# Half of the inner index of two column groups of each output projection by seven half products

## The chip, the cores and the metric

The kernel runs on one core of one Trainium2 chip. The metric is the time of one execution on the device in microseconds (us); the time before is the median of three runs. Profiled executions are taken separately; the trace of one of them gives every time below that isn't called a median.

## What is computed

The reference is a decoder trunk of two layers on 256 tokens of width 2048 in float32. Layer 0 mixes the tokens by gated linear attention, layer 1 by attention over a sliding window; each also attends to 256 memory tokens, and each has an MLP of width 8192:

```python
for i in range(DEPTH):
    h = rmsnorm(x, attn_norm_g[i])
...
    x = x + jnp.concatenate([o_mix, o_mem], axis=-1) @ w_out[i]
    x = x + squared_relu_mlp(rmsnorm(x, mlp_norm_g[i]), w_up[i], w_down[i])
return rmsnorm(x, final_norm_g)
```

Here `o_mix` is 256 x 1536, from the layer's mixer, and `o_mem` 256 x 512, from the memory; `DEPTH` is 2. The change concerns the product with `w_out[i]`: 256 tokens, an inner index of 2048 and 2048 columns.

## The kernel before

All weights pass through a list of *items*, made layer by layer (projections of the mixer, `out_halves`, `mlp_halves`). An item is one 128 x 1024 block of weights in float32 with the matmuls that use it. The main loop walks the list with a lead: at item i, SP issues the load of item i+13 (`load`, into one of eight buffers `wr`), item i+7 may add blocks on DVE (`prep`), and item i+5 is split (`split`, L1141): ACT copies the block in reduced precision to `wh` (L1152), DVE writes the rest to `wl` (L1153). There are six buffers, here called slots, for each of `wh` and `wl`. Then come late tasks (normalisations, adds into `x`) and the item's own matmuls. A matmul product is made of three: high by high, high by low, low by high, each 128x512.

The engines run their own queues in order. The order that stands in each queue is fixed when the program is built, from the order of this code and a scheduler's own model of times; a buffer's next writer waits for its last reader, whichever comes last.

`out_halves` (L805) makes the output projection in four column groups g of 512 columns, each of eight items (parts) of two chunks of the inner index, that is 2 token tiles x 2 chunks x 3 = 12 matmuls. The order is group 0 parts 0 to 5, group 1 parts 0 to 5, the rest of both, then group 2 and group 3. The left operands are `os0` to `os15`, high and low parts of the attention's output. `OUT_ROWS` gives the order of the chunks. When a group has ended, `add_residual` (L772) adds its two accumulators into x (`x02` is token tile 0, group 2) on DVE (L774), and `norm_task` begins the norm that the MLP needs.

The MLP's `down_fast` already uses seven products in place of eight for its down projection: for a 2 x 2 arrangement of blocks (token tiles by inner halves, and inner halves by column groups) it multiplies operands made on DVE by sums of weight blocks, in an order given by `FAST` (L61), and adds the results into x with signs (each entry: left operand, name, accumulator, whether it is that accumulator's first, and the uses):

```python
A21, A11, A22, A12, S3, GG, S2, S4 = range(8)
FAST = [(A11, "B11", 0, True, [(0, 0, 1)]),
        (GG, "T1", 1, True, [(1, 1, -1)]),
        (S2, "T2", 0, False, [(0, 1, -1)]),
        (S4, "B22", 1, False, [(0, 1, -1)]),
        (S3, "T3", 0, False, [(1, 1, -1)]),
        (A12, "B21", 1, True, [(0, 0, 1)]),
        (A22, "T4", 0, False, [(1, 0, 1)])]
```

T1 to T4 are sums of blocks: a room `sum` takes B11, gets B12 added (T1), then B22 (T2) and B21 (T4) by loads that POOL issues and that add in place; a room `b12` takes B12 and gets B22 added for T3. A *half product* is one such product for one half of its inner part (u=0 or 1): two chunks, six matmuls.

The names in the attention's phase: `mk` and `mv` hold the memory's keys and values, `v` the mixer's values in layer 0, `wp` and `wpt` attention weights in layer 1.

Of the kernel before, what the change touches and what calls it, by code (L numbers as in the profile page):

```python
# [10 lines left out]
F32 = mybir.dt.float32  # L11
F32R = mybir.dt.float32r
AF = mybir.ActivationFunctionType
ALU = mybir.AluOpType
# [56 lines left out]
WOVEN_MEM = [3, 3, 2, 2, 2, 1, 0]  # L71

# [17 lines left out]
def trunk_kernel(ctx: ExitStack, tc: tile.TileContext, a, out):  # L90
# [358 lines left out]
    def gla_halves():  # L449
        hs = []  # L450

        def v_done(g):
            def f(accs):
                if g == 0:
                    S["v"] = S["phase"].pool.tile([P, 2, 1536], F32, name="v")
                for t in range(2):
                    w = min(388, 1536 - g * 388)
                    act.activation(S["v"][:, t, g * 388:g * 388 + w], accs[t][:, 0:w], AF.Copy,
                                   scale=S["st"].tok[:, t:t + 1])
                    if w < 388:  # L460
                        act.activation(glr_tok[:, t, 0:16], accs[t][:, w:388], AF.Copy, scale=S["st"].tok[:, t:t + 1])
                if g == 3:
                    tasks.append(gate_task())
            return f
# [81 lines left out]
    def gla_task(h):  # L546
# [57 lines left out]
        for j in range(3):  # L604
            b = bank("aux", f"go{h}{j}")
            col = h * 384 + j * P
            pe.matmul(b[:, 0:T], S["v"][:, 0, col:col + P], at[:, 0:T], start=True, stop=False, skip_group_check=True)
            pe.matmul(b[:, P:T], S["v"][:, 1, col:col + P], at[:, T:T + P], start=False, stop=True,
# [202 lines left out]

    def out_halves(layer):
        hs = []
        for g in range(4):
            def done(accs, g=g):
                add_residual(g, accs)
                tasks.append(norm_task(g, f"mx{layer}", G_MLP + layer))

            hs.append(tm_halves(f"o{layer}{g}", [a["w_out"][layer, g, i] for i in range(8)], 512, lambda: S["os"], done,
                                OUT_ROWS[layer]))  # L820

        return hs[0][0:6] + hs[1][0:6] + hs[0][6:] + hs[1][6:] + hs[2] + hs[3]

    def mlp_halves(layer):
# [5 lines left out]
        def open_phase():  # L830
            S["phase"].close()
            S["phase"] = Phase(f"mlp{layer}")
            S["st"].finish()

        def up(n):
# [3 lines left out]
            def part(i):  # L839
                def mm(wh, wl):  # L840
                    if i == 0:
                        if n == 0:
                            open_phase()
                        st["acc"] = [bank("main" if n < 2 else "aux", f"u{layer}{n}_acc{t}") for t in range(2)]
                    for t in range(2):
                        for k in range(2):
# [4 lines left out]
                            pe.matmul(acc, hi, h, start=2 * i + k == 0, stop=False)  # L851
                            pe.matmul(acc, hi, l, start=False, stop=False)  # L852
                            pe.matmul(acc, lo, h, start=False, stop=2 * i + k == NK - 1)  # L853
                    if i == 7:
# [7 lines left out]
            return [part(i) for i in range(8)]  # L862
# [52 lines left out]
        sums, held = {}, {}  # L915

        def down_fast(e):
# [5 lines left out]
            def item(idx, u, pair):  # L923
                o, name, which, first, uses = FAST[idx]

                def mm(wh, wl):
                    if u == 0 and pair not in sums:
                        sums[pair] = {}
                    if u == 0 and which not in sums[pair]:
                        sums[pair][which] = bank("main", f"d{layer}{e}{pair}{which}")  # L930
                    acc = sums[pair][which]
                    products(acc, 2 * e + u, o, wh, wl, first and u == 0, u == 1)
                    if u == 1:
                        def take():
                            for t, col, sign in uses:
                                dst = x[t][2 * pair + col]
                                if sign > 0:
                                    dve.tensor_tensor(dst, acc, dst, ALU.add)  # L938
                                else:
                                    dve.tensor_tensor(dst, dst, acc, ALU.subtract)  # L940
                                if e == 7 and name in ("T3", "T4"):
                                    tasks.append(norm_end_task(2 * pair + col))
                        later.append([1, take])

                def tile_of(kind):
                    return lambda *_: held[kind, pair, u, e]

                def new(kind):
                    def f():
                        held[kind, pair, u, e] = S["phase"].pool.tile([P, 1024], F32, tag=f"{kind}{pair}{u}",  # L950
                                                                   name=f"{kind}{layer}{e}{pair}{u}")
                        return held[kind, pair, u, e]
                    return f

                def plus(other):
                    return lambda raw: pool_e.dma_start(held["sum", pair, u, e], block(pair, u, other), accum_op=ALU.add)  # L956

                def first_sum():
                    dve.tensor_tensor(held["sum", pair, u, e], held["sum", pair, u, e], held["b12", pair, u, e], ALU.add)

                def third_sum(raw):
                    dve.tensor_tensor(held["b12", pair, u, e], held["b12", pair, u, e], raw, ALU.add)

                if name == "B11":
                    return Item(block(pair, u, "B11"), 1024, mm=mm, into=new("sum"), tile=tile_of("sum"))
                if name == "T1":
                    return Item(block(pair, u, "B12"), 1024, mm=mm, into=new("b12"), tile=tile_of("sum"),
                                prep=first_sum, then=plus("B22"))
                if name == "T2":
                    return Item(None, 1024, mm=mm, tile=tile_of("sum"), then=plus("B21"))  # L970
                if name == "T4":
                    return Item(None, 1024, mm=mm, tile=tile_of("sum"))
                if name == "T3":
                    return Item(None, 1024, mm=mm, tile=tile_of("b12"))
                if name == "B22":
                    return Item(block(pair, u, "B22"), 1024, mm=mm, then=third_sum)
                return Item(block(pair, u, name), 1024, mm=mm)

            return [item(idx, u, pair) for idx in range(7) for u in range(2) for pair in range(2)]


# [107 lines left out]
        def woven(us, ds, counts):  # L1089

            hs = []
            for i, d in enumerate(ds):
                w, j = counts[i // 4], i % 4
                for _ in range((w * (j + 1) + 3) // 4 - (w * j + 3) // 4):
                    hs += us.pop(0)
                hs.append(d)
            return hs

        first, second = up(0), up(1)

# [162 lines left out]
```

## Time and profile before

| | us |
|---|---|
| median of three runs (2059.42 to 2059.82) | 2059.75 |
| profiled execution | 2060.74 |
| its span in the trace | 2058.6 |
| groups 2 and 3 of layer 0's output projection (16 items) | 374.9 to 418.4 |
| the same of layer 1 | 1331.0 to 1374.5 |

PE is the matmul engine, PEld its weight loads, DVE, ACT and POOL the vector, scalar and GpSimd engines, SP issues loads. The span is what the trace covers; 2.1 us lie around it. A timeline row gives start and duration of an instruction in us, engine, line, operation, output and inputs; in square brackets stands the idle time before it on its engine and what ended it. Matmuls overlap, so the step from start to start is what one holds PE for.

### The profile page before, as it was taken

Reading aid. Unit: us, or ns where it says so; the run is one execution under the profiler, and the core shown is the slowest. Engines: PE = TensorE matmul, PEld = TensorE weight load, DVE = VectorE, ACT = ScalarE, POOL = GpSimd, SP = SyncE. Lnnn points to the kernel's source line nnn. Section 1 sums busy time; section 2 is a strip of 40 time slices with the busy share of each in tenths; the row PEclk is TensorE's granted clock in tenths of the full one; section 3 lists DMA queues with packets and bytes.
Section 4 is the critical chain, followed back from the end, with each engine's and each line's share of the span. In section 5 each row is a group of like instructions: output and inputs, shape, how many; then the busy total and the mean of one; then the engine's idle time right before and its main releaser. Section 6 shows DMA issues by size and latency. Waiting matters only on the chain.

```text
span 2058.6 us, 27262 instructions
## 1 busy us (share of the span) xinstructions
PE 2046.6 (99%) x9870; PEld 1718.9 (83%) x9870; DVE 1652.7 (80%) x1985; ACT 1268.8 (62%) x1664; POOL 119.2 (6%) x162
## 2 busy tenths in 40 slices
PE   9999999999999999999999999999999999999998
PEld 9988888888888888888888888888888888888887
DVE  6667775558889898898998677656898998988986
ACT  7656665546666756666567566555666666666663
POOL 0100000001011010010100000000010100101000
PEclk9999999999999999999999999999999999999999
DMA  9955555577798897988997644575988979879772
GB/s 333 372 172 171 175 164 167 183 254 186 259 277 231 274 241 239 278 222 267 281 282 256 197 133 131 167 230 180 277 230 269 249 233 280 217 266 267 230 236 96
DMA packets 133462, 472.00 MB, mean 229 GB/s; under 512 B 15196, under 2 KB 15408, under 8 KB 133328
## 3 DMA queue, kind: packets, MB, share of 16 engines
q1 hardware_dynamic: 113040, 399.16, 57.0%
q0 software_dynamic: 18752, 67.20, 17.7%
q10 hardware_dynamic: 1536, 3.91, 0.5%
q8 instruction: 77, 1.26, 0.2%
q14 instruction: 57, 0.47, 0.1%
HBM read 462.68 MB, written 7.34 MB: 228 GB/s over the span
## 4 chain that ended last, share of the span: by engine, by line
PE 95%; DVE 2%; DMA 2%; ACT 1%; issue 0%; DVEq 0%; ACTq 0%
PE u_acc L852 11%; PE u_acc L853 11%; PE u_acc L851 11%; PE d L911 9%; PE d L913 9%; PE d L912 9%; PE p_acc L211 6%; PE s_acc L211 3%; PE o_acc L237 3%; PE o_acc L239 3%; PE o_acc L238 3%; PE p_acc L212 3%; PE s_acc L212 2%; PE h L876 1%; PE v_acc L237 1%; PE v_acc L239 1%
## 5 line engine op out<-in xcount | busy, mean ns | idle before, releaser
L1152 ACT ACTIVATE wh<-wr 128x1024 fp32r<-128x1024 f32 (+1 forms) x618 | 644.9, 1048 | 537.0 <-PE u_acc L853 241.6
L1153 DVE TENSOR_TENSOR wl<-wr,wh 128x1024 fp32r<-128x1024 f32 (+1 forms) x618 | 742.8, 1209 | 263.4 <-ACT wh L1152 258.4
L851 PE MATMUL u_acc<-wh,mx 128*128 128x512 f32 x1024 | 399.1, 390 | 0.0
L853 PE MATMUL u_acc<-wh,mx 128*128 128x512 f32 x1024 | 398.6, 389 | 0.0
L852 PE MATMUL u_acc<-wl,mx 128*128 128x512 f32 x1024 | 398.4, 389 | 0.0
L911 PE MATMUL d<-wh,hid 128*128 128x512 f32 x840 | 331.0, 394 | 0.4 <-ACT hid L890 0.4
L913 PE MATMUL d<-wh,hid 128*128 128x512 f32 x840 | 326.8, 390 | 0.5 <-DVE hid L892 0.3
L912 PE MATMUL d<-wl,hid 128*128 128x512 f32 x840 | 326.8, 389 | 0.0
L1152 ACT ACTIVATE wh<-sum 128x1024 fp32r<-128x1024 f32 x240 | 252.6, 1059 | 108.9 <-PE u_acc L853 52.9
L1153 DVE TENSOR_TENSOR wl<-sum,wh 128x1024 fp32r<-128x1024 f32 x240 | 289.8, 1220 | 32.8 <-ACT wh L1152 32.0
L853 PEld LDWEIGHTS u_acc<-wh,mx 128*128 128x128 f32 x1024 | 192.2, 188 | 40.1
L851 PEld LDWEIGHTS u_acc<-wh,mx 128*128 128x128 f32 x1024 | 192.2, 188 | 39.9
L852 PEld LDWEIGHTS u_acc<-wl,mx 128*128 128x128 f32 x1024 | 192.2, 188 | 39.8
L956 POOL DMA_DIRECT2D sum<-in_w_down_dram x120 | 102.8, 857 | 1529.9 <-DVE wl L1153 1027.4
L911 PEld LDWEIGHTS d<-wh,hid 128*128 128x128 f32 x840 | 157.7, 188 | 36.6 <-DVE x L938 3.7
L913 PEld LDWEIGHTS d<-wh,hid 128*128 128x128 f32 x840 | 157.7, 188 | 34.7 <-DVE hid L892 1.3
L912 PEld LDWEIGHTS d<-wl,hid 128*128 128x128 f32 x840 | 157.9, 188 | 31.3
L211 PE MATMUL p_acc<-ax,wh 128*128 128x512 f32 x512 | 182.0, 399 | 0.0
L212 PE MATMUL p_acc<-ax,wl 128*128 128x256 f32 x512 | 142.7, 279 | 0.0
L211 PEld LDWEIGHTS p_acc<-ax,wh 128*128 128x128 f32 x512 | 96.0, 188 | 21.5
L211 PE MATMUL s_acc<-ax,wh 128*128 128x512 f32 x304 | 110.5, 405 | 0.0
L237 PE MATMUL o_acc<-wh,os 128*128 128x512 f32 x256 | 100.9, 394 | 0.0
(268 smaller groups left out, 2592.5 us busy)
## 6 DMA issues: line engine op xcount, KB each, us to landing
wr<-in_w_up_dram SPq DMA_DIRECT2D x256, 512.0 KB, 4.5
wr<-in_w_down_dram SPq DMA_DIRECT2D x136, 512.0 KB, 5.7
sum<-in_w_down_dram POOLq DMA_DIRECT2D x120, 512.0 KB, 7.6
wr<-in_w_gla_dram SPq DMA_DIRECT2D x64, 512.0 KB, 3.7
wr<-in_w_out_dram SPq DMA_DIRECT2D x64, 512.0 KB, 3.6
sum<-in_w_down_dram SPq DMA_DIRECT2D x60, 512.0 KB, 5.0
b<-in_w_down_dram SPq DMA_DIRECT2D x60, 512.0 KB, 5.0
wr<-in_w_swa_dram SPq DMA_DIRECT2D x38, 512.0 KB, 4.0
```

Of the source, the lines that this page charges most:

```text
L211: pe.matmul(acc, wh[:, k * P:(k + 1) * P], rk, start=kk == 0, stop=False, skip_group_check=True)
L212: pe.matmul(acc[:, T:2 * T], wl[:, k * P:(k + 1) * P], rk[:, 0:T], start=False, stop=kk == NK - 1, skip_group_check=True)
L237: pe.matmul(acc, hi, h, start=first, stop=False)
L851: pe.matmul(acc, hi, h, start=2 * i + k == 0, stop=False)
L852: pe.matmul(acc, hi, l, start=False, stop=False)
L853: pe.matmul(acc, lo, h, start=False, stop=2 * i + k == NK - 1)
L911: pe.matmul(acc, hi, h, start=first and c == 0, stop=False, skip_group_check=True)
L912: pe.matmul(acc, hi, l, start=False, stop=False, skip_group_check=True)
L913: pe.matmul(acc, lo, h, start=False, stop=last and c == 1, skip_group_check=True)
L956: return lambda raw: pool_e.dma_start(held["sum", pair, u, e], block(pair, u, other), accum_op=ALU.add)
L1152: act.activation(hi[i][:, 0:w], r[:, 0:w], AF.Copy)
L1153: dve.tensor_tensor(lo[i][:, 0:w], r[:, 0:w], hi[i][:, 0:w].bitcast(F32), ALU.subtract)
```

## The change

Of each output projection, groups 0 and 1 stay as they are. Of groups 2 and 3, the inner half with parts 0 to 3 is made by seven products for the two groups together (for each of two halves u, so fourteen half products), and parts 4 to 7 stay plain items, called `p0` to `p3` (group 3) and `p4` to `p7` (group 2). The order, by `FAST_OUT` and `WOVEN_OUT`, is: p0, B11u0, p1, B11u1, p2, T1u0, p3, T1u1, p4, B22u0, p5, B22u1, p6, T2u0, T2u1, p7, T3u0, T3u1, B21u0, B21u1, T4u0, T4u1. These are 22 items in place of 16.

The left operands are made by a task that starts with the projection's first item: for each u, four DVE adds of a high and a low part to `q` (128x2x128 each), four DVE differences to `z` (128x256), four ACT copies to `left` (high parts; `left10` to `left13` are S3, GG, S2, S4 of u=1) and four DVE low parts. `sum` of u=0 and u=1 takes the room of `mk` and `mv`. In layer 0, `b12` takes `v2` (u=0) and `v0` (u=1), `q` takes `v0` and `z` takes `v1`, for which `v` is divided into three tiles; in layer 1, `b12` and `q` take the two buffers of `wp` and `z` that of `wpt`. The MLP's first two groups of `up` read their chunks in the order 0, 1, 2, 3, 6, 7, 4, 5, and the norm's `finish` is called before the fifth item of `up`. The function `seven` is the body of `down_fast` moved out, with places for rooms, blocks and operands.

```diff
+FAST_OUT = [0, 1, 3, 2, 4, 5, 6]
+WOVEN_OUT = [2, 2, 2, 1, 1, 0, 0]
...
-                    S["v"] = S["phase"].pool.tile([P, 2, 1536], F32, name="v")
+                    S["v"] = [S["phase"].pool.tile([P, 2, 512], F32, tag=f"v{i}", name=f"v{i}") for i in range(3)]
...
+    def seven(label, pairs, order, sums, block, mult, room, ended):
...
+            if name == "B11":
+                return Item(block(pair, u, "B11"), 1024, mm=mm, into=new("sum"), tile=tile_of("sum"))
+            if name == "T1":
+                return Item(block(pair, u, "B12"), 1024, mm=mm, into=new("b12"), tile=tile_of("sum"),
+                            prep=first_sum, then=plus("B22"))
+            if name == "T2":
+                return Item(None, 1024, mm=mm, tile=tile_of("sum"), then=plus("B21"))
+            if name == "T4":
+                return Item(None, 1024, mm=mm, tile=tile_of("sum"))
+            if name == "T3":
+                return Item(None, 1024, mm=mm, tile=tile_of("b12"))
+            if name == "B22":
+                return Item(block(pair, u, "B22"), 1024, mm=mm, then=third_sum)
+            return Item(block(pair, u, name), 1024, mm=mm)
+
+        return [item(idx, u, pair) for idx in order for u in range(2) for pair in pairs]
...
+        def operands_task():
+
+            for _ in range(5):
+                yield
+            for u in range(2):
+                q = scratch("v0" if layer == 0 else "wp").rearrange("p (o c) -> p o c", o=4)
+                z = scratch("v1" if layer == 0 else "wpt").rearrange("p (o c) -> p o c", o=4)
+                for half in range(2):
+                    for c in range(2):
+                        r = S["os"][rows[4 * u + 2 * half + c]]
+                        dst = q.rearrange("p (h t) c -> p h t c", h=2)[:, half, :, c * P:(c + 1) * P]
+                        dve.tensor_tensor(dst, r[:, 0:T].bitcast(F32).rearrange("p (t c) -> p t c", t=2),
+                                          r[:, T:2 * T].bitcast(F32).rearrange("p (t c) -> p t c", t=2), ALU.add)
+                yield
+
+                dve.tensor_tensor(z[:, 0, :], q[:, 0, :], q[:, 1, :], ALU.subtract)
+                dve.tensor_tensor(z[:, 1, :], q[:, 3, :], q[:, 1, :], ALU.subtract)
+                dve.scalar_tensor_tensor(z[:, 2, :], z[:, 1, :], -1.0, q[:, 0, :], ALU.mult, ALU.subtract)
+                dve.scalar_tensor_tensor(z[:, 3, :], z[:, 2, :], -1.0, q[:, 2, :], ALU.mult, ALU.subtract)
+                yield
+                for i, o in enumerate((S3, GG, S2, S4)):
+                    c = 8 + 4 * u + i
+                    left[u, o] = sp.tile([P, 2 * T], F32R, tag=f"A{c}", name=f"o{layer}left{u}{i}")
+                    act.activation(left[u, o][:, 0:T], z[:, i, :], AF.Copy)
+                yield
+                for i, o in enumerate((S3, GG, S2, S4)):
+                    dve.tensor_tensor(left[u, o][:, T:2 * T], z[:, i, :], left[u, o][:, 0:T].bitcast(F32), ALU.subtract)
+                yield
...
+        def room(kind, pair, u):
+            if kind == "sum":
+                return scratch(("mk", "mv")[u])
+            return scratch(("v2", "v0")[u] if layer == 0 else "wp")
...
+        hs = [out_group(g, list(range(8)), normed) for g in range(2)]
+
+        hs = hs[0][0:6] + hs[1][0:6] + hs[0][6:] + hs[1][6:]
+        plain = out_group(3, [4, 5, 6, 7], lambda g: None) + out_group(2, [4, 5, 6, 7], lambda g: None)
+        return hs + woven([[z] for z in plain], seven(f"o{layer}", [1], FAST_OUT, {}, block, mult, room, ended), WOVEN_OUT)
...
+        first, second = [up(n, [0, 1, 2, 3, 6, 7, 4, 5]) for n in range(2)]
```

The following rows show what stands in an engine's queue; line numbers in rows of the changed kernel are its own (L1269 and L1270 are the splits to `wh` and `wl`, L781 the add of a plain group into x, L944 the adds to `q`, L948 to L951 the differences to `z`, L956 and L959 the high and low parts of `left`, L911 to L913 plain matmuls, L971 to L973 those of a half product).

DVE in layer 0, at the end of group 2 of the projection, in the kernel before:

```order
L1153 TENSOR_TENSOR wl_3945<-wr_3741,wh_3944 128x1024
L1153 TENSOR_TENSOR wl_3963<-wr_3764,wh_3962 128x1024
L774 TENSOR_TENSOR x02_174<-o02_acc0_3816,x02_174 128x512
L774 TENSOR_TENSOR x12_303<-o02_acc1_3817,x12_303 128x512
L1153 TENSOR_TENSOR wl_3983<-wr_3806,wh_3982 128x1024
L1153 TENSOR_TENSOR wl_4007<-wr_3830,wh_4006 128x1024
```

And where group 2 ends in the changed kernel (`o_v2` and `o_v0` are the rooms of `b12`; `wl_4059` belongs to T3u0, `wl_4071` to T3u1, and `q` is `o_v0_3701`, `z` is `o_v1_3702`):

```order
L1270 TENSOR_TENSOR wl_4059<-o_v2_3647,wh_4058 128x1024
L781 TENSOR_TENSOR x02_174<-o02_acc0_4010,x02_174 128x512
L781 TENSOR_TENSOR x12_303<-o02_acc1_4011,x12_303 128x512
L1270 TENSOR_TENSOR wl_4071<-o_v0_3695,wh_4070 128x1024
L944 TENSOR_TENSOR o_v0_3701<-os4_2443 128x2x128
L944 TENSOR_TENSOR o_v0_3701<-os5_2525 128x2x128
L944 TENSOR_TENSOR o_v0_3701<-os6_2833 128x2x128
L944 TENSOR_TENSOR o_v0_3701<-os7_2903 128x2x128
L948 TENSOR_TENSOR o_v1_3702<-o_v0_3701 128x256
L949 TENSOR_TENSOR o_v1_3702<-o_v0_3701 128x256
L950 SCALAR_TENSOR_TENSOR o_v1_3702<-o_v1_3702,o_v0_3701 128x256
L959 TENSOR_TENSOR o0left10_3747<-o_v1_3702,o0left10_3747 128x256
```

The adds to `q` for u=1 now stand behind the split of T3u1, the last reader of the room that they write. On ACT the same place reads, in the changed kernel (`wh_4070` is T3u1, `wh_4088` B21u0):

```order
L1269 ACTIVATE wh_4040<-wr_3914 128x1024
L1269 ACTIVATE wh_4058<-o_v2_3647 128x1024
L1269 ACTIVATE wh_4070<-o_v0_3695 128x1024
L956 ACTIVATE o0left10_3747<-o_v1_3702 128x256
L956 ACTIVATE o0left11_3749<-o_v1_3702 128x256
L956 ACTIVATE o0left12_3751<-o_v1_3702 128x256
L956 ACTIVATE o0left13_3753<-o_v1_3702 128x256
L1269 ACTIVATE wh_4088<-wr_3960 128x1024
```

In the kernel before, ACT has at the end of group 2:

```order
L1152 ACTIVATE wh_3944<-wr_3741 128x1024
L1152 ACTIVATE wh_3962<-wr_3764 128x1024
L1152 ACTIVATE wh_3982<-wr_3806 128x1024
L153 ACTIVATE mx0_sq_3986,mx0_ss_3747<-x02_174 128x512
L153 ACTIVATE mx0_sq_3988,mx0_ss_3747<-x12_303 128x512
```

The four copies to `left` of u=1 have come between the splits of T3u1 and B21u0, where before there was a split for every item in turn.

DVE in layer 1 at the same place, before:

```order
L1153 TENSOR_TENSOR wl_12137<-wr_11933,wh_12136 128x1024
L1153 TENSOR_TENSOR wl_12155<-wr_11956,wh_12154 128x1024
L774 TENSOR_TENSOR x02_174<-o12_acc0_12008,x02_174 128x512
L774 TENSOR_TENSOR x12_303<-o12_acc1_12009,x12_303 128x512
L1153 TENSOR_TENSOR wl_12175<-wr_11998,wh_12174 128x1024
L1153 TENSOR_TENSOR wl_12199<-wr_12022,wh_12198 128x1024
```

And in the changed kernel, where `wl_12324` is T3u0, `wl_12336` T3u1, `q` is `o_wp_11966`, a buffer of `wp`, and `z` is `o_wpt_11967`:

```order
L1270 TENSOR_TENSOR wl_12306<-wr_12179,wh_12305 128x1024
L1270 TENSOR_TENSOR wl_12324<-o_wp_11896,wh_12323 128x1024
L781 TENSOR_TENSOR x02_174<-o12_acc0_12275,x02_174 128x512
L944 TENSOR_TENSOR o_wp_11966<-os0_11085 128x2x128
L944 TENSOR_TENSOR o_wp_11966<-os1_11088 128x2x128
L944 TENSOR_TENSOR o_wp_11966<-os2_11266 128x2x128
L944 TENSOR_TENSOR o_wp_11966<-os3_11269 128x2x128
L948 TENSOR_TENSOR o_wpt_11967<-o_wp_11966 128x256
L949 TENSOR_TENSOR o_wpt_11967<-o_wp_11966 128x256
L1270 TENSOR_TENSOR wl_12336<-o_wp_11960,wh_12335 128x1024
L950 SCALAR_TENSOR_TENSOR o_wpt_11967<-o_wpt_11967,o_wp_11966 128x256
L959 TENSOR_TENSOR o1left10_12012<-o_wpt_11967,o1left10_12012 128x256
```

Here the adds to `q` stand behind the split of T3u0, and the split of T3u1 has come between the second and the third difference.

PE in layer 0, from group 3's last item but one to its last, before:

```order
L237 MATMUL o03_acc1_3991<-wh_4006,os9_3314 128x512
L238 MATMUL o03_acc1_3991<-wl_4007,os9_3314 128x512
L239 MATMUL o03_acc1_3991<-wh_4006,os9_3314 128x512
L237 MATMUL o03_acc0_3990<-wh_4046,os10_3400 128x512
L238 MATMUL o03_acc0_3990<-wl_4047,os10_3400 128x512
L239 MATMUL o03_acc0_3990<-wh_4046,os10_3400 128x512
```

And from the end of `p7` (`wh_4040`) in the changed kernel, where `wh_3916` is T1u1, `wh_4026` T2u1 and `wh_3943` B22u0:

```order
L912 MATMUL o02_acc1_4011<-wl_4041,os11_3480 128x512
L913 MATMUL o02_acc1_4011<-wh_4040,os11_3480 128x512
L971 MATMUL o011_3967<-wh_3916,o0left11_3749 128x512
L972 MATMUL o011_3967<-wl_3917,o0left11_3749 128x512
L973 MATMUL o011_3967<-wh_3916,o0left11_3749 128x512
L971 MATMUL o011_3967<-wh_3916,o0left11_3749 128x512
L972 MATMUL o011_3967<-wl_3917,o0left11_3749 128x512
L973 MATMUL o011_3967<-wh_3916,o0left11_3749 128x512
L971 MATMUL o010_3907<-wh_4026,o0left12_3751 128x512
L972 MATMUL o010_3907<-wl_4027,o0left12_3751 128x512
L973 MATMUL o010_3907<-wh_4026,o0left12_3751 128x512
L971 MATMUL o011_3967<-wh_3943,o0left03_3659 128x512
```

Behind `p7` now follows T1u1 with the left operand `left11`, then half of T2u1; in the whole program PE has 9324 rows where it had 9348.

More of the change, by code (lines that the diff above doesn't have):

```diff
@@ L921, in block @@
                 return wd[layer, e, 2 * pair + int(name[2]) - 1, 2 * u + int(name[1]) - 1]
[L923 to L977, printed above, removed]
@@ L982, in mlp_halves @@
+            return seven(f"d{layer}{e}", range(2), range(7), sums, block, mult, room, ended)
         LAST = [(14 + i // 2, (A11, A21) if i % 2 == 0 else (A12, A22)) for i in range(4)]
```

153 lines of the change are left out of this document (121 added, 32 removed).

## Prediction

> **What bounds the kernel now.** I read the page first, then PE's waits, then the stage that is changed.
>
> ```profile
> span 2058.6 us, 27262 instructions
> PE 2046.6 (99%) x9870; PEld 1718.9 (83%) x9870; DVE 1652.7 (80%) x1985; ACT 1268.8 (62%) x1664; POOL 119.2 (6%) x162
> PE 95%; DVE 2%; DMA 2%; ACT 1%; issue 0%; DVEq 0%; ACTq 0%
> ...
> PE warm L129 <- DVE ones L119: 1.1, 1, 1.1
> PE glr_ps L542 <- ACT glr_tok L461: 1.1, 2, 0.8
> ```
>
> PE is busy for 99% of the span and makes 95% of the chain that ended last. The longest of its waits is 1.1 us, in the whole kernel. So a matmul removed is time saved, and a wait put on PE is time added, with next to no slack to take it up. The windows of the last 16 items of the two output projections (groups 2 and 3) say the same:
>
> ```profile
> 374.90:418.40 43.50, 43.50 (x201) 36.17 (x201) 24.04 (x27) 21.27 (x31) 0.00 (x0) 1.00 0.57 181
> 1331.00:1374.50 43.50, 43.50 (x202) 36.17 (x201) 24.02 (x27) 21.03 (x30) 0.00 (x0) 1.00 0.60 181
> ```
>
> After the span the columns are PE, PEld, DVE, ACT, POOL, the granted clock, the DMA share and GB/s: PE has no gap, DVE is half empty, the DMA engines 40% empty. There is room for more work on both; the question is its order.
>
> **What goes.** One item's twelve matmuls, from the first of one item to the first of the next:
>
> ```profile
> 402.38 0.39 PE L238 MATMUL o_acc<-wl,os 128*128 128x512 f32 x1
> ...
> 405.10 0.39 PE L238 MATMUL o_acc<-wl,os 128*128 128x512 f32 x1
> 407.36 0.39 PE L239 MATMUL o_acc<-wh,os 128*128 128x512 f32 x1
> ```
>
> Twelve steps take 2.72 us, so a matmul holds PE for 0.2267 us; its 0.39 overlaps the next. A plain item is 2.72, a half product (six matmuls) 1.36. In each projection eight plain items become fourteen half products: 96 matmuls become 84. Twelve fewer are 2.72 us, and both layers give **-5.44 us**. The shape and operand kinds are those of the plain items, so I expect no new pace.
>
> **What a split costs.** The rows at an item's end in the steady state, where the slot it frees is filled again:
>
> ```profile
> 407.79 1.06 ACT L1152 ACTIVATE wh<-wr 128x1024 fp32r<-128x1024 f32 x1 [1.66 <-PE o_acc L239]
> ...
> 408.88 1.23 DVE L1153 TENSOR_TENSOR wl<-wr,wh 128x1024 fp32r<-128x1024 f32 x1 [1.49 <-ACT wh L1152]
> ```
>
> The item's last matmul starts at 407.36, so the next item may start at 407.59; `wh` starts 0.20 later, `wl` 1.09 after `wh`, and it lasts 1.23. With 0.05 to reach PE (my estimate), a freed slot is usable 0.20 + 1.09 + 1.23 + 0.05 = 2.57 us after its last matmul. The other work of DVE and ACT that I need:
>
> ```profile
> 394.41 1.22 DVE L1153 TENSOR_TENSOR wl<-wr,wh 128x1024 fp32r<-128x1024 f32 x1 [1.54 <-ACT wh L1152]
> 395.55 1.28 DVE L774 TENSOR_TENSOR x<-o_acc,x 128x512 f32<-128x512 f32 x2
> ...
> 320.51 0.42 DVE L513 TENSOR_TENSOR sg<-p_t,sg 128x256 f32<-128x256 f32 x1
> 320.85 0.42 DVE L142 TENSOR_TENSOR os<-xo,os 128x256 fp32r<-128x256 f32 x1
> ...
> L774 DVE TENSOR_TENSOR x<-o_acc,x 128x512 f32<-128x512 f32 x16 | 10.4, 682 | 0.0
> L141 ACT ACTIVATE os<-sg 128x256 fp32r<-128x256 f32 x12 | 4.9, 409 | 2.3 <-DVE sg L514 2.3
> L959 DVE TENSOR_TENSOR sum<-sum,b 128x1024 f32<-128x1024 f32 x60 | 73.2, 1220 | 0.2
> ```
>
> In a full DVE queue `wl` takes 1.14 (394.41 to 395.55), a 128x512 add 0.60 (two in 1.28, one lasting 0.68), a 128x256 operation 0.34 (320.51 to 320.85), lasting 0.42. An ACT copy of 128x256 lasts 0.41.
>
> **What comes: waits on PE.** I laid the order of the changed program against these durations, item by item.
>
> Layer 0, the large one. When `p7` (the last plain item) runs, the six slots hold `p7`, T1u1, T2u1, B22u0, B22u1 and T3u0; the last five are split, but PE reaches them only through T1u1, whose operand `left11` doesn't exist yet. The split of T3u1 (`wh_4070`) therefore takes the slot of `p7`, and the four adds that make `q` for u=1 write `o_v0`, the room that `wl_4071` is just reading. PE has nothing meanwhile. From the end of `p7`: 0.20, `wh` 1.09, `wl` 1.23 gives 2.52; four adds of 0.34 give 3.88; z0 0.34 and z1 0.42 give 4.64; `left10` holds ACT 0.08 longer, `left11` 0.41 and 0.05 to PE: PE starts at 5.18. T1u1's third matmul needs `lo11`; z2, `left10`'s low part and z3 at 0.34 each and `lo11` at 0.42 end at 6.08, usable at 6.13, of which two matmuls (0.45) are done: **5.68 us** in all.
>
> Layer 1 has `q` in a room of its own size (`o_wp_11966`) whose last reader is `wl_12324` (T3u0), which was over before. The adds start with the 128x512 add of `p7`'s first accumulator, 0.93 before `p7` ends (five matmuls, 1.13, follow that accumulator's last one, less 0.20): 0.60 for it, four adds, z0 and z1 end their turns at 1.71. There `wl_12336` stands ahead of z2 in DVE's queue, 1.14, then z2, low part, z3 and `lo11`: 1.71 + 1.14 + 3 x 0.34 + 0.42 = 4.29, usable at 4.34. PE does four matmuls (0.91) of T1u1 and T2u1 in that time: **3.43 us**.
>
> The smaller ones, both layers alike unless said. `p4` waits for the add that frees the accumulator of group 3; it stands behind `wl` (`wl_3977`) whose slot T1u0 freed one plain item before: 0.20 + 1.09 + 1.14 + 0.68 + 0.05 = 3.16 against 2.72, so 0.44. `p7`'s slot is that of `p6`, with only T2u0 (1.36) and `p7`'s first two matmuls (0.45) between: 2.57 - 1.81 = 0.76. B22u0 needs the add of x13 behind T1u1: 0.20 + 0.68 + 0.05, less three matmuls of T2u1 (0.68), 0.25; in layer 1 that add stands behind two low parts and the add of x12 and ends at 6.17 after `p7`, usable at 6.22 against 4.34 + 8 x 0.2267 = 6.15 on PE, 0.07. B21u0 needs x03 subtracted, which stands behind the `wl` (`wl_4102`, in layer 1 `wl_12379`) whose slot B22u0 frees: the same 3.16 after B22u0's end, in which PE has B22u1 (1.36) and in layer 0 three matmuls of T2u1 besides: 1.12 and 1.80.
>
> Layer 0: 0.44 + 0.76 + 5.68 + 0.25 + 1.12 = 8.25. Layer 1: 0.44 + 0.76 + 3.43 + 0.07 + 1.80 = 6.50. Together 14.75.
>
> **What I cost at nothing.** The twelve further splits and eight 128x1024 sums (1.22 each) lie in the half-empty time of DVE and ACT shown above, or in the items before it, and those that delay anything are counted in the waits above. The eight accumulating loads:
>
> ```profile
> sum<-in_w_down_dram POOLq DMA_DIRECT2D x120, 512.0 KB, 7.6
> ```
>
> They land 7.6 us after issue; the shortest distance from a `wl` that lets one go to the `wh` that needs it is 14.4 us by the schedule. If that cover went, the price would be what is lacking; POOL has nothing else to do there. In SP's queue a load into a room waits for the room's last reader, and the loads behind it wait too: the first stands at item 4 (`mk`), the one into `o_v0` at item 10, four items (10.9 us) behind the last reader of u=0's `q`, so none waits long against a lead of 13 items. Dividing `v` adds four small ACT copies, none ahead of `glr_tok`, and moving `finish` and the order of `up` changes no count. If the cover for these failed, I bound each at one split chain, 2.57.
>
> Not shown anywhere is an add with a 128x2x128 pattern. I take the 128x256 row (0.34). At the 128x512 row's 0.60, eight adds on the path give 2.1 us more; at nothing, 2.7 less. Both ends stay in the range.
>
> **Sum.** The profiled execution took 2060.74 us (span 2058.6 and 2.1 around it). 2060.74 + 14.75 - 5.44 = 2070.05. The median of the runs, 2059.75, is 0.99 lower, so the time is **2069.1 us**, 0.45% slower.
>
> **Rivals.**
> 1. *The matmuls decide, faster:* u=1's operands are ready early and the small waits vanish in lookahead. It gives 2059.75 - 5.44 = 2054.3. It would need all waits below 1.3 us to come out over 0.2% (4.1 us, about what a measurement here can tell from no change). Against it: `wl_4071` must read `o_v0` before the adds write it, a dependency of data, not of pace. 3%.
> 2. *Only the two long waits are real, no change:* the small ones, 5.64, are my sums of queue places and could be taken up by PE's order. 5.68 + 3.43 - 5.44 = +3.67, 2063.4. For it: in the trace of before PE waits for nothing here. Against it: the half products halve the cover of each split. 10%.
> 3. *PE's clock falls in the gap.* The start of the kernel shows a slow pace:
>
> ```profile
> 6.23 2.02 PE L237 MATMUL v_acc<-wh,ax 128*128 128x388 f32 x4 [0.47 <-ACT wh L1152]
> 8.05 0.53 PE L238 MATMUL v_acc<-wl,ax 128*128 128x388 f32 x1
> ...
> 9.99 0.53 PE L239 MATMUL v_acc<-wh,ax 128*128 128x388 f32 x1
> 10.31 0.50 PE L237 MATMUL v_acc<-wh,ax 128*128 128x388 f32 x1
> ...
> 11.88 0.34 PE L238 MATMUL v_acc<-wl,ax 128*128 128x388 f32 x1
> ...
> 12.59 0.34 PE L239 MATMUL v_acc<-wh,ax 128*128 128x388 f32 x1
> ```
>
>    Six steps from 8.05 to 9.99 are 0.323 each, four from 11.88 to 12.59 are 0.178. The slow pace lasts from 6.23 to about 10.31, 4.1 us; were it paid again after the 5.18 us gap, it would cost 4.1 x (1 - 0.178/0.323) = 1.84: 2070.9, and 2072.7 for both layers. Before, no gap within the kernel is over 1.1 us, so nothing decides it. 27%.
>    [...]
> 4. *After-effects:* the emptied lookahead lets the first items of the MLP wait once for a split chain: + 2.57, 2071.6. For it: norm, loads and splits of `up` come within 20 us of the gap. Against it: those loads are issued 13 items ahead and are not held by PE. 8%.
>
> That the change doesn't do what it says is excluded: PE's order has 24 matmuls fewer.
>
> **How the numbers follow.** The forecast, 2069.1, has 52%; the rivals 3, 10, 27 and 8. Faster by over 0.2% is rival 1 (0.03), within 0.2% rival 2 (0.10), slower the rest (0.87). The range of 2063.0 to 2073.5 holds all but the first rival and a part of the fourth with a clock loss on top.
>
> **What would show it.** After `p7` in each layer, a PE gap of about 5.2 and 2.3 us ended by ACT `left` and further ones by DVE; `wh` of T3u1 0.2 us behind `p7`; 24 fewer PE matmuls; in the slice a granted clock below 1 if rival 3 is right. I am wrong if PE runs T1u1 directly behind `p7`, or if the list of PE's waits names a DMA.

## The result and the profile after

| | us |
|---|---|
| changed kernel, median of 6 runs (2070.57 to 2078.01) | 2075.5 |
| kernel before, median of 6 runs beside it (2058.7 to 2062.54) | 2059.78 |
| ratio, with its 95% interval | 1.007 (1.006 to 1.008) |
| profiled execution of the changed kernel | 2075.8 |
| its span | 2074.1 |

The change makes the kernel 15.7 us slower by the medians, 0.8%. Forecast were 9.3 us more, 2069.1, with a range up to 2073.5. From here on line numbers in rows are those of the kernel named. First the page of the changed kernel (span, busy times) and its list of PE's waits (total, times, longest):

```profile
span 2074.1 us, 27369 instructions
PE 2047.7 (99%) x9846; PEld 1715.5 (83%) x9846; DVE 1697.6 (82%) x2067; ACT 1285.8 (62%) x1696; POOL 125.7 (6%) x170
...
PE o L971 <- ACT o0left L956: 5.0, 1, 5.0
PE o L971 <- ACT o1left L956: 2.8, 2, 2.1
PE o L971 <- DVE x L840: 2.8, 2, 1.7
PE glr_ps L549 <- ACT glr_tok L468: 2.3, 2, 1.9
...
PE o_acc L912 <- DVE wl L1270: 1.1, 2, 0.5
PE o_acc L911 <- DVE x L781: 0.8, 2, 0.4
```

The new waits are there, each at its place: `left` of layer 0 and of layer 1, the subtraction of x03 in both, `wl` of p7, the add that frees p4's accumulator. But one number contradicts the sum: PE has 24 matmuls fewer, worth 5.4 us, and yet its busy time has grown from 2046.6 to 2047.7. Its matmuls have become longer somewhere. The granted clock, the share of its full clock that PE is given, shows where. Of all windows of 10 us with matmuls in them, these four have one that isn't 1.00 (the column that reads 0.83, 0.95, 0.70, 0.83):

```profile
80.00:90.00 10.00, 7.75 (x37) 6.33 (x36) 4.91 (x8) 8.07 (x18) 0.00 (x0) 0.83 1.02 414
400.00:410.00 10.00, 4.48 (x18) 2.93 (x17) 7.90 (x14) 4.00 (x6) 0.53 (x1) 0.95 0.60 139
410.00:420.00 10.00, 8.94 (x26) 6.48 (x27) 5.77 (x10) 4.68 (x6) 0.00 (x0) 0.70 0.18 57
1370.00:1380.00 10.00, 7.46 (x24) 5.26 (x24) 8.32 (x14) 5.65 (x8) 0.00 (x0) 0.83 0.17 50
```

Two are the gaps behind p7; the first, at 80 us, is in the first projection of layer 0. The timeline of PE in the changed kernel, behind p7 of layer 0:

```profile
404.34 0.40 PE L913 MATMUL o_acc<-wh,os 128*128 128x512 f32 x1
409.73 0.79 PE L971 MATMUL o<-wh,o0left 128*128 128x512 f32 x1 [4.99 <-ACT o0left L956]
410.32 0.63 PE L972 MATMUL o<-wl,o0left 128*128 128x512 f32 x1
...
415.60 0.54 PE L972 MATMUL o<-wl,o0left 128*128 128x512 f32 x1
415.98 0.40 PE L973 MATMUL o<-wh,o0left 128*128 128x512 f32 x1
416.21 0.39 PE L971 MATMUL o<-wh,o0left 128*128 128x512 f32 x1
```

From start to start, 404.34 to 409.73, less one matmul of 0.23, PE stands for 5.16 us (forecast 5.18). Then fourteen steps take 6.25 us (409.73 to 415.98), 0.38 to 0.59 each where 0.227 is the full pace; fourteen at full pace are 3.17. In layer 1:

```profile
1368.24 0.40 PE L913 MATMUL o_acc<-wh,os 128*128 128x512 f32 x1
1370.71 0.50 PE L971 MATMUL o<-wh,o1left 128*128 128x512 f32 x1 [2.08 <-ACT o1left L956]
1371.06 0.40 PE L972 MATMUL o<-wl,o1left 128*128 128x512 f32 x1
1372.18 0.80 PE L971 MATMUL o<-wh,o1left 128*128 128x512 f32 x1 [0.73 <-ACT o1left L956]
1372.78 0.63 PE L972 MATMUL o<-wl,o1left 128*128 128x512 f32 x1
...
1375.21 0.40 PE L971 MATMUL o<-wh,o1left 128*128 128x512 f32 x1
...
1380.66 0.47 PE L971 MATMUL o<-wh,os 128*128 128x512 f32 x1 [1.75 <-DVE x L840]
```

The gap is 2.47 - 0.23 = 2.24 us (forecast 2.3), and the slow pace comes here too, from 1372.18 to 1375.21, seven steps. Behind the wait of 1.75 us it doesn't come: the steps from 1380.66 on are 0.23 to 0.30.

Where the 15.5 us of span arise is read from marks that both programs pass: the first matmul of layer 0's projection (329.55 against 327.78 before) and one copy out of `u_acc` in the middle of each MLP. Kernel before:

```profile
746.97 0.69 ACT L857 ACTIVATE p<-u_acc,mx_r 128x512 f32<-128x512 f32 x1 [0.30 <-PE u_acc L853]
...
1491.96 0.69 ACT L857 ACTIVATE p<-u_acc,mx_r 128x512 f32<-128x512 f32 x1 [0.30 <-PE u_acc L853]
```

Changed kernel:

```profile
329.55 0.39 PE L911 MATMUL o_acc<-wh,os 128*128 128x512 f32 x1
...
756.86 0.69 ACT L1030 ACTIVATE p<-u_acc,mx_r 128x512 f32<-128x512 f32 x1 [0.30 <-PE u_acc L1026]
...
1507.84 0.69 ACT L1030 ACTIVATE p<-u_acc,mx_r 128x512 f32<-128x512 f32 x1 [0.30 <-PE u_acc L1026]
```

| stretch | forecast | in the traces |
|---|---|---|
| up to layer 0's projection | 0 | 1.77 |
| from there to layer 0's MLP | 8.25 - 2.72 = 5.53 | 9.89 - 1.77 = 8.12 |
| from there to layer 1's MLP | 6.50 - 2.72 = 3.78 | 15.88 - 9.89 = 5.99 |
| rest | 0 | 15.5 - 15.88 = -0.4 |

So 6.2 us are missing in the forecast: 2.6 and 2.2 in the projections, 1.8 ahead of them, and 0.4 less behind them.

### The profile page after: what moved, and what is told of

Same layout as the page of the kernel before. It is cut to its first block, busy times and chain, and to the rows that moved or that the text cites. A ratio compares the mean times of both kernels' runs of the same rounds, so it can differ in the third digit from the quotient of the medians.

```text
span 2074.1 us, 27369 instructions
## 1 busy us (share of the span) xinstructions
PE 2047.7 (99%) x9846; PEld 1715.5 (83%) x9846; DVE 1697.6 (82%) x2067; ACT 1285.8 (62%) x1696; POOL 125.7 (6%) x170
## 4 chain that ended last, share of the span: by engine, by line
PE 95%; DVE 2%; DMA 1%; ACT 1%; issue 0%; SPq 0%; DVEq 0%; ACTq 0%
PE u_acc L1026 11%; PE u_acc L1025 11%; PE u_acc L1024 11%; PE d L1084 9%; PE d L1086 9%; PE d L1085 9%; PE p_acc L214 6%; PE s_acc L214 3%; PE p_acc L215 3%; PE o_acc L912 2%; PE o_acc L911 2%; PE o_acc L913 2%; PE s_acc L215 2%; PE h L1049 1%; DVE wl L1270 1%; PE v_acc L242 1%
## 5 line engine op out<-in xcount | busy, mean ns | idle before, releaser
L1269 ACT ACTIVATE wh<-wr 128x1024 fp32r<-128x1024 f32 (+1 forms) x610 | 635.8, 1048 | 510.6 <-PE u_acc L1026 233.0
L1270 DVE TENSOR_TENSOR wl<-wr,wh 128x1024 fp32r<-128x1024 f32 (+1 forms) x610 | 732.5, 1209 | 219.9 <-ACT wh L1269 211.9
L1269 ACT ACTIVATE wh<-sum 128x1024 fp32r<-128x1024 f32 x240 | 252.6, 1059 | 108.4 <-PE u_acc L1026 52.9
L1270 DVE TENSOR_TENSOR wl<-sum,wh 128x1024 fp32r<-128x1024 f32 x240 | 290.0, 1222 | 32.7 <-ACT wh L1269 32.4
L215 PEld LDWEIGHTS p_acc<-ax,wl 128*128 128x128 f32 x512 | 97.3, 190 | 0.3
```

Source lines behind the costliest of these rows:

```text
L215: pe.matmul(acc[:, T:2 * T], wl[:, k * P:(k + 1) * P], rk[:, 0:T], start=False, stop=kk == NK - 1, skip_group_check=True)
L1269: act.activation(hi[i][:, 0:w], r[:, 0:w], AF.Copy)
L1270: dve.tensor_tensor(lo[i][:, 0:w], r[:, 0:w], hi[i][:, 0:w].bitcast(F32), ALU.subtract)
```

## The experiments

**The operands earlier, in both layers and in one.** The task that makes the left operands waits a number of items before it starts; two in place of five put `q` of u=1 ahead of the loads that take its room.

```diff
-            for _ in range(5):
+            for _ in range(2):
```

> The task that makes the left operands waits 2 items instead of 5, so q of u=1 is made before the load of its room's next user is issued; nothing else is changed. Theory (waits on PE and the slow pace behind them are the whole loss): the gaps of 4.99 and 2.08 us behind p7 go, and with the half products in their own turn the slots refill in time too; 14.8 us of waits and some 5 us of slow pace go, and only the 24 matmuls are left: 2059.8 - 5.4 = 2054.3, between 2053.3 and 2055.8. Rival A (only the two long waits go, the small ones stay: 5.6 us, and no slow pace): 2054.3 + 5.6 = 2059.9. Rival B (the twelve splits, eight sums and eight loads more are not free): over 2057 with no wait over 1 us in the two projections.

Measured: 2053.98 (2051.56 to 2055.91, 6 runs) against 2059.44 before, ratio 0.9971 (0.9959 to 0.9982). The waits of its PE are only those that the kernel before has as well:

```profile
PE v_acc L240 <- ACT wh L1269: 1.8, 2, 1.1
PE glr_ps L549 <- ACT glr_tok L468: 1.4, 2, 1.0
PE warm L132 <- DVE ones L122: 1.1, 1, 1.1
PE wt L719 <- DVE wp L711: 0.4, 1, 0.4
PE d L1084 <- ACT hid L1063: 0.4, 2, 0.2
```

No wait in the projections, not even the small ones, and the 24 matmuls come out as time. That the medians give 5.46 us for 5.44 is in part luck: the interval reaches from 3.7 to 8.4 us. The two stretches of its trace, read at the marks above, are sharper: 3.1 and 2.8 us shorter than before, for 2.72 each. Rivals A and B fall; the twelve splits, the sums and the loads cost nothing that these runs can tell. In layer 0 alone (`range(2 if layer == 0 else 5)`):

> The same, in layer 0 alone; layer 1 waits 5 items as in the changed kernel. Theory: layer 0 saves 8.25 us of waits and about 2.9 us of slow pace (13 to 14 matmuls at a step of 0.43 in place of 0.227): 2075.5 - 11.2 = 2064.3, and the PE gap behind p7 of layer 1 stays at 2.1 us with a slow pace behind it. Rival (the slow pace is a state of the run and not caused by the gap): 2075.5 - 8.25 = 2067.3, with matmuls at the slow step still somewhere in layer 0's projection.

Measured: 2061.89 (2060.63 to 2064.97, 10 runs), 2.4 below what the theory gave and 5.4 below the rival. Its trace has the 2.1 and 1.7 us waits of layer 1, with the slow pace behind the first, and none in layer 0's projection. That layer 1 alone costs 2061.89 - 2053.98 = 7.9 us fits its own 5.99 + 2.72 = 8.7 in the traces. In layer 0 the saving in the traces is what the theory gave: the stretch falls from 427.31 to 416.03 us, by 11.3. The 2.4 lie ahead of it: layer 0's projection starts at 327.10 here and at 329.55 in the trace of the changed kernel.

**One item, or the early start?** With 4 and 2 items in the two layers:

```diff
-            for _ in range(5):
+            for _ in range(4 if layer == 0 else 2):
```

> The operands' task waits 4 items in layer 0 and 2 in layer 1 (5 and 5 in the changed kernel). Theory (what decides is only whether q of u=1 takes its room before the load of b12 of u=1, issued at item 10 in layer 0, and of b12 of u=0 in layer 1, issued at item 8): no wait of PE over 1 us in either projection, the time that of the kernel with 2 and 2 items, 2054 within 2. Rival (an early start is what counts): waits of 1 us and more behind p7 in layer 0.

Measured: 2053.25 in one run, and no wait of PE in either projection. In layer 0 a start one item earlier is enough: what decides is who takes the room `v0` first, at item 9 the operands or at item 10 the load. The traces show that order: here the second four adds to `q` start from 238.3 to 279.6 us and the load into their room is issued at 332.9; in the changed kernel the load is issued at 279.6 and the adds start at 407.1.

**The side parts alone.** Plain items in all groups, with `v` in three tiles, the new order of `up` and the new place of `finish`:

```diff
-                        if (g, i) == (0, 0):
-                            tasks.append(operands_task())
...
-        hs = [out_group(g, list(range(8)), normed) for g in range(2)]
+        hs = [out_group(g, list(range(8)), normed) for g in range(4)]
...
-        plain = out_group(3, [4, 5, 6, 7], lambda g: None) + out_group(2, [4, 5, 6, 7], lambda g: None)
-        return hs + woven([[z] for z in plain], seven(f"o{layer}", [1], FAST_OUT, {}, block, mult, room, ended), WOVEN_OUT)
+        return hs[0][0:6] + hs[1][0:6] + hs[0][6:] + hs[1][6:] + hs[2] + hs[3]
```

> The changed kernel with plain items in all four column groups: v in three tiles, the order of up and the place of finish are as in the change, but no half products and no left operands are made. Theory (these side parts are free): 2059.8, within 1.0 us. Rival (the wait for glr_tok, 1.91 us in the changed kernel against 0.76, and the slow pace behind it come from the divided v): 2059.8 + 1.8 = 2061.6, and matmuls at the slow step between 84 and 89 us.

Measured: 2060.02 against 2059.44, ratio 1.0006 (0.9996 to 1.0015), but in two groups: six runs from 2058.4 to 2060.3 and four from 2063.0 to 2065.5. The traced one was the slowest, 2065.45, with 2.4 us of wait for `glr_tok`. So it was run again beside the kernel before:

> The kernel with the side parts alone, beside the kernel before. Theory (the side parts are free): the same median as the kernel before within 1 us. Rival (the divided v makes the long wait for glr_tok more frequent): a median 2 us and more above it.

> The kernel before once more with its own trace. Its runs so far lie in two groups, near 2059 and near 2062. Theory (the wait for glr_tok, set by when the loads of the memory's tokens land, is longer in some runs, and over about 1.4 us it brings a slow pace, whatever the kernel): about a third of the runs 2 to 3 us above the others, and if the traced run is one of them, a wait of 1.4 us and more for glr_tok and slow matmuls behind it. Rival (only the kernels with the divided v have it): all runs within 1 us of 2059.4, the wait at 0.8 us or less.

Measured: 2060.46 with the side parts, ratio 1.0002 (0.9993 to 1.0011), and 2059.91 for the kernel before against itself, 0.9999 (0.999 to 1.0008); 11 runs each, from 2058.31 to 2063.85 and from 2058.16 to 2062.85. The side parts are free by the median. Of the expectation for the kernel before only a half came true: its runs spread by 4.7 us as well, but the traced one, 2061.66, has a wait for `glr_tok` of 0.8 us and no slow pace behind it (granted clock 1.00 from 80 to 90 us). It does have a slow pace at its start: the granted clock is 0.91 over the first 20 us. Slow pace behind `glr_tok` was seen only in traces with the divided `v` (three of nine, with a granted clock of 0.83 to 0.85 from 80 to 90 us, against none of four without). There PE's two waits for it add up to between 1.2 and 2.8 us, without the division to between 0.7 and 1.2. So whether the division lengthens the wait stays open; the medians show no difference.

**Gaps of PE in the kernel before.** To see what idle time alone does, chains of DVE operations that leave all values as they are were put behind two items of group 2, where the next item must wait for them (`GAPS` is `[[9, 2], [11, 4]]`, and `[[14, 7], [7, 1]]` in the second):

```diff
+        def gap(item, seen, due, k):
+            mm = item.mm
+
+            def f(wh, wl):
+                mm(wh, wl)
+                rows = OUT_ROWS[layer]
+                r, d = S["os"][rows[seen]][:, T:2 * T], S["os"][rows[due]][:, T:2 * T]
+                for j in range(k):
+                    dve.tensor_tensor(r, r.bitcast(F32), r.bitcast(F32), ALU.max)
+                dve.scalar_tensor_tensor(d, r.bitcast(F32), 0.0, d.bitcast(F32), ALU.mult, ALU.add)
+            item.mm = f
+
+        for (g, i), k in zip([(2, 2), (2, 7)], GAPS[layer]):
+            gap(hs[g][i], 2 * i + 1, 2 * ((i + 1) % 8), k)
```

> The kernel before with chains of small DVE operations put between items of group 2 so that PE waits: by the order and the durations of the rows about 2.4 and 1.9 us in layer 0, 3.2 and 3.2 us in layer 1, with smaller waits of 0.4 to 0.9 beside them, 15.0 us in all. Theory (a gap of about 2 us or more is followed by matmuls at a step of 0.43 us for 3 to 6 us): the time is 15.0 + 4 x 1.2 to 2.9 us above the kernel before, 2080 to 2086, with slow matmuls behind three or four of the gaps. Rival 1 (the slow pace needs a gap as long as layer 0's 5 us): 2074.8, no slow matmul. [...]

> The kernel before with waits put into group 2 as in the first gap kernel: by the order and row durations about 4.5 and 4.8 us in layer 0, and 1.6 and 1.2 us in layer 1, with smaller ones beside them, 16.3 us in all. Theory (the slow pace follows a gap from 1.7 us or so on): slow matmuls for 5 to 6 us behind each of the two large gaps, 2.5 to 3 us each, none or few in layer 1: 2059.4 + 16.3 + 5 to 6 = 2081 to 2082. Rival (any gap over 1 us brings them): slow matmuls in layer 1 too, 2083 or more.

Measured, one run each: 2084.77 (the kernel before beside it 2059.44) and 2083.26 (2061.49). In the first all four gaps are followed by steps of 0.43 us, for 3.7 to 5.6 us. In the second the two large ones are, and in layer 1 the larger of the two that I had called harmless:

```profile
1353.95 0.39 PE L240 MATMUL o_acc<-wl,os 128*128 128x512 f32 x1
1354.58 0.73 PE L239 MATMUL o_acc<-wh,os 128*128 128x512 f32 x2 [0.24 <-ACT wh L1169]
1356.01 0.73 PE L240 MATMUL o_acc<-wl,os 128*128 128x512 f32 x2 [0.69 <-DVE wl L1170]
1358.18 0.68 PE L241 MATMUL o_acc<-wh,os 128*128 128x512 f32 x1 [1.44 <-DVE os L833]
1358.66 0.63 PE L239 MATMUL o_acc<-wh,os 128*128 128x512 f32 x1
```

Three waits of 0.24, 0.69 and 1.44 us with four matmuls between them, and the pace is slow from 1358.18 to 1361.9. The theory's threshold of 1.7 us for one wait falls, by this trace and not by the time: 2083.26 is 21.8 above its own kernel before, which the theory's 21.3 to 22.3 would allow. A single wait of 1.75 us, as shown above, doesn't bring the slow pace, these three close together do. The two gap kernels hold no half product, so idle time of PE was enough for it here.

**The changed kernel with PE kept busy.** Matmuls that nobody reads are put into PE's waits, so that it runs on while ACT and DVE make the operands:

```diff
+FILL = [27, 17]
...
+                    if (g, i) == (2, 7):
+                        b = bank("aux", f"o{layer}fill")
+                        for j in range(FILL[layer]):
+                            pe.matmul(b, left[0, GG][:, 0:P], left[0, S3], start=True, stop=True)
```

> The changed kernel with 27 and 17 further matmuls (layer 0, layer 1) into a buffer that nothing reads, which stand in PE's queue in the places where it waited: in p7, behind p7 and before T2u1. The end of the waits is set by ACT and DVE as before, so by the order and the row durations the time at which PE goes on doesn't move; only PE's idle time goes. Theory (beside 14.8 us of waits, the changed kernel pays a slow pace that idle time brings): no matmul at the step of 0.43 us behind p7 and about 4 to 5 us less than the changed kernel, 2070 to 2071.5. Rival (the slow matmuls are made by something else, such as power or the half products themselves): the slow steps stay and the time stays at 2075.5, or grows.

> The changed kernel again, beside the filled one on the same chip: 2075.5 as before, within 1.5 us. If it comes out near 2071 in most runs, the place at which slow pace begins changes from run to run and the filled kernel must be compared with that.

Measured side by side, 5 runs each: 2071.61 filled (2069.08 to 2071.91), ratio to before 1.0049 (1.0035 to 1.0063); 2073.94 not filled (2072.54 to 2074.94), ratio 1.0063 (1.005 to 1.0075). The intervals overlap, the runs don't. The timeline of PE in the filled kernel behind p7 of layer 0, with the end of the operands at the same place:

```profile
403.54 0.40 PE L914 MATMUL o_acc<-wh,os 128*128 128x512 f32 x1
403.77 5.15 PE L921 MATMUL o0fill<-o0left,o0left 128*128 128x512 f32 x22
408.94 0.50 PE L976 MATMUL o<-wh,o0left 128*128 128x512 f32 x1
409.27 0.40 PE L977 MATMUL o<-wl,o0left 128*128 128x512 f32 x1
```

T1u1 comes 5.40 us behind p7's last matmul, as without the filling (5.39), but goes on at full pace (granted clock 1.00 from 400 to 420 us, where the changed kernel has 0.95 and 0.70). Without PE's idle time the kernel is 2.3 us faster, and what is left is 2071.61 - 2061.49 (before, on that chip) = 10.1 us, where the forecast had 9.3 for waits less matmuls. The changed kernel beside it is 2073.94 - 2061.49 = 12.5 us slower than before, where the first comparison gave 15.7. A part of the slow pace was hidden: the wait for the subtraction of x03 in layer 0 is 1.06 us in the changed kernel and 1.72 in the filled one.

**The faster version once more.**

> The kernel whose operands are made after 2 items, again: 5.4 us below the kernel before, 2054 where that has 2059.4, within 1.5. Rival (the first session was a lucky chip): a ratio whose interval reaches 0.999 or more.

Measured: 2053.66 (5 runs) against 2060.48, ratio 0.9968 (0.9955 to 0.998). It beats the kernel before as well as the changed one.

**The same stretches in every trace.** The medians differ by a microsecond or two for reasons that lie elsewhere, above all ahead of the projection. The two stretches from the marks above (first matmul of layer 0's projection, copy in layer 0's MLP, copy in layer 1's MLP) agree to about 0.5 us between two traces of one kernel:

| traces | layer 0, us | layer 1, us |
|---|---|---|
| kernel before, two | 419.19, 419.05 | 744.99, 745.18 |
| side parts alone, two | 419.01, 419.06 | 745.51, 744.99 |
| changed kernel, two | 427.31, 426.92 | 750.98, 750.69 |
| changed and filled | 425.31 | 749.38 |
| operands early in layer 0 alone | 416.03 | 750.78 |
| operands early, two | 416.05, 416.21 | 742.15, 742.43 |
| operands after 4 and 2 items | 416.25 | 742.52 |

## Why the prediction fell short

*What goes* was right: 5.44 us for 24 matmuls, and 5.46 by the medians, 5.6 to 6.0 in the two stretches, appeared when nothing stood against it.

*The waits* were right in place and size. The reason of the long ones, that `wl` of T3u1 reads the room that the adds must write and itself waits for p7's slot, is what the early start takes away. The rows of DVE behind p7 of layer 0 in the changed kernel follow the working:

```profile
405.86 1.23 DVE L1270 TENSOR_TENSOR wl<-o_v,wh 128x1024 fp32r<-128x1024 f32 x1 [0.40 <-ACT wh L1269]
407.12 1.43 DVE L944 TENSOR_TENSOR o_v<-os 128x256 f32<-128x256 f32 x4
408.47 0.42 DVE L948 TENSOR_TENSOR o_v<-o_v 128x256 f32<-128x256 f32 x1
```

The four adds whose pattern no row of before had take 1.35 us from 407.12 to 408.47, 0.34 each: the 128x256 row was the right end. Sizes of the other waits, from start to start less one matmul: 5.16 for 5.18, 2.24 for 2.3; 1.91 and 1.22 at L840 for 1.80 and 1.12; 0.70 each for 0.76 at p7. The 1.12 came out right by luck: with PE at full pace, in the filled kernel, that wait is 1.88.

*What I cost at nothing* (splits, sums, loads, SP's queue, side parts) did cost nothing: the stretches with the operands early and with the side parts alone say so. The claim for the side parts has the one exception left open above.

*The step that failed is the forecast's choice against rival 3.* The sum lets PE go on at full pace behind each gap. That had 52%, a fall of the clock 27%. The runs show the slow pace behind both gaps, in both traces of the changed kernel. Its price in layer 0 is 6.25 - 3.17 = 3.08 us, of which 0.50 would have been wait for `lo11` anyway: 2.6, which is the whole surplus of that stretch. In layer 1 the twelve matmuls of T1u1 and T2u1 with their waits run from the end of p7, 1368.47, to 1375.92, 7.45 us; less 2.72 of work and 3.50 of forecast waits, 1.2 us are slow pace. (By its own steps, seven in 3.03 us for 1.59, it is 1.4, and the waits are 0.2 shorter than forecast.) The other 1.0 us of that stretch isn't placed; between the second traces of the two kernels it is 0.5. Without idle time, in the filled kernel, the two stretches are 1.6 and 1.3 us shorter than in the trace of the changed kernel beside it, 2.9 in all; the medians give 2.3, and the filled kernel has a slow pace of its own at 84 us. The rival's own price, 2 x 1.84 = 3.7 us from the start of the kernel, is near the sum of 2.6 and 1.2, but not right in its parts: the slow pace lasted longer in layer 0 than in layer 1.

How much idle time brings the slow pace, the trace of before couldn't say: its longest wait is 1.1 us. Its start showed two paces alone, 0.323 and 0.178 us a step (128x388). The runs show two of a ratio of 1.9, 0.43 against 0.227 (128x512): the pace fell behind waits of 2.08 and 0.73 us, in layer 1 of the changed kernel, and behind 0.24, 0.69 and 1.44 in the second gap kernel. In the changed kernel the half clock comes in stretches of 3.41 us on one grid, as the last section shows.

*The range* failed with that and with a term put at nothing. It ended at 2073.5, and the case of both layers slow gave 2072.7, to which the 1.8 us ahead of the projection came. The trace of the changed kernel had started faster and stood 1.0 us ahead of that of before between 40 and 60 us; it lost 2.7 us at the wait for `glr_tok`:

```profile
83.43 0.28 PE L549 MATMUL glr_ps<-ident,glr_tok 128*16 128x128 f32 x1 [1.91 <-ACT glr_tok L468]
84.06 0.28 PE L549 MATMUL glr_ps<-ident,glr_tok 128*16 128x128 f32 x1 [0.35 <-ACT glr_tok L468]
...
85.34 0.41 PE L215 MATMUL p_acc<-ax,wl 128*128 128x256 f32 x1
85.55 0.63 PE L214 MATMUL p_acc<-ax,wh 128*128 128x512 f32 x1
```

PE waits 1.91 us here, where the longest such wait in the trace of before is 0.8, and goes on slowly (granted clock 0.83 from 80 to 90 us). In the second trace of the changed kernel (span 2072.2) that wait is 0.8 and no slow pace follows (1.00 in the same 10 us), so the change doesn't always bring it.

## What to carry to other kernels

A buffer that serves two purposes in turn is a place in a queue: whether the small early use or the long late one takes it first was one item of the order in layer 0, and over both layers it decided between 5.5 to 6.8 us faster and 12 to 16 us slower. Where such a reuse puts work behind a split whose slot is itself behind the work, the chain can be added up from rows of the trace, and it came out within 4% at the two long gaps. To idle time of a PE that was never idle before, add what it costs to get up to pace again, here 3.1 us behind the gap of 5.16 and 1.2 behind that of 2.24.

## What the runs showed of the hardware

Behind idle time PE stepped at 0.43 us in place of 0.227, for 3.0 us in layer 1 of the changed kernel and 6.2 in layer 0; the spell cost 1.2 us there and 3.1 here. In the changed kernel it followed the waits of 4.99, of 2.08 and 0.73, and of 1.91 and 0.35 us; in the first gap kernel, among others, those of 0.34, 0.16 and 1.66, in the second those of 0.24, 0.69 and 1.44, and in the filled kernel at 84 us those of 1.37 and 0.35. It didn't follow the single ones of 1.06 and 1.75 in the changed kernel, nor those of 1.72 and 1.75 in the filled one.

The clock records of the changed kernel's trace show where the spells lie. Until the last matmul the half clock (0.50) comes three times, from 84.82 and 1371.64 us for 3.413 us and from 409.08 for two such in a row (6.827). The starts lie whole multiples of 3.413 us apart, the second 95.0 and the third 377.0 stretches behind the first. These are windows on this grid; the columns after the length are PE's busy time and the granted clock, then the DMA share and GB/s:

```profile
81.40:84.82 3.42, 1.17 (x8) 1.00 1.03 420
84.82:88.23 3.41, 3.41 (x13) 0.50 1.02 419
405.67:409.08 3.41, 0.00 (x0) 1.00 0.09 37
409.08:415.91 6.83, 6.18 (x14) 0.50 0.00 0
1368.23:1371.64 3.41, 1.14 (x4) 1.00 0.56 181
1371.64:1375.06 3.42, 2.88 (x7) 0.50 0.00 0
1378.47:1381.88 3.41, 1.66 (x7) 1.00 0.84 270
```

The filled kernel, and windows of the same length in the second trace with the side parts alone, which stayed at full clock:

```profile
80.68:84.09 3.41, 1.69 (x10) 1.00 1.00 402
84.09:87.51 3.42, 3.42 (x13) 0.50 1.03 422
...
81.08:84.50 3.42, 1.79 (x10) 1.00 1.02 418
84.50:87.91 3.41, 3.41 (x21) 1.00 1.03 423
```

In the changed kernel the three stretches with 2.25, 3.41 and 2.27 us of idle time, added up over their waits, are followed by half clock; the one with 1.75, the wait at L840 in layer 1, isn't (granted clock 1.00 from 1380 to 1390 us). In the filled kernel 1.72 us is followed by it, in the second trace with the side parts 1.63 isn't. The slow steps do not always begin at the end of the gap: in layer 1 of the changed kernel two matmuls at 1370.71 and 1371.06 still take 0.50 and 0.40, the half clock begins at 1371.64, and the next matmul, at 1372.18, takes 0.80.
